# Gate projections of a hybrid layer: made among the attention heads and kept in DRAM, in place of all together behind them

## Chip, cores and metric

The program runs on one core of a Trainium2 chip (trn2). The metric is the device time of the whole program in microseconds: 1872.27 us in the kernel before, the median of three runs (1864.81 to 1877.15).

## What is computed

Two transformer blocks run one after the other on 512 tokens of width 1024, in float32. The change lies in the first half of the first block, which mixes tokens in two ways and weighs them with two gates:

```python
n = rmsnorm(h, g_mix)
z = n @ w_in                                     # 1024 -> 3*1536 + 512 + 2*1024
q, k, v, u = ...                                 # 12 heads of 128, and u of 512 channels
gate_attn = sigmoid(z[..., o2:o2 + 1024])
gate_ssm = sigmoid(z[..., o2 + 1024:o2 + 2048])
# 3 groups of 4 heads with dilations 1, 4 and 16; causal band in each; joined by their log-sums
attn_d = joined_heads @ w_attn_proj              # 512 -> 1024
y = gelu(s5_ssm(u, ...))                         # 32 groups of 16 channels, 64 complex states each
ssm_d = (y @ w_glu_a) * sigmoid(y @ w_glu_b)
h = h + (gate_attn * attn_d + gate_ssm * ssm_d) @ w_out
```

The feed-forward of block 1, the per-layer embedding and all of block 2 follow; the change does not touch them.

## The kernel before

Activations lie transposed, 128 channels by 512 tokens to a tile. Each float32 product is made of three matmuls on TensorE (PE): every operand is split into a high part, copied by ScalarE (ACT, L122), and a low part, the difference, made by VectorE (DVE, L123). `mm` (L159 to L161) issues high x high, high x low, low x high; where a row reads `mm<-y0h,wh`, the projection's input tile 0 meets the weight tile. One projection (`proj`) of 8 input tiles to 128 output channels is 24 matmuls of 512 columns. `weights` (L139 to L153) loads the 128 x 1024 weights of one projection into one of three buffers `wr` (L150) on the DMA queue of SyncE (SP), and splits them into one of two pairs `wh`/`wl`; the load and the split are given a priority 40 steps ahead of the place where they are called (`WLEAD`). A scheduler orders each engine's instructions by such priorities; each queue, SP's too, is served in order.

Block 1 first makes y (the input times the gain, split), u and the tables. Then four rounds `h` run `attention_1`, one head of each of the three groups in each: per group `qk_tile` for q and for k (projection, rotary embedding on DVE and GpSimd (POOL), split), a projection for v, its transposition (L703), scores (`sc`), masks and maxima, exponentials (L659 and L726 wait for such steps); at the end softmax weights, transposes of the probabilities (L736) and their products with v (`po`, L748; the copy into `attn` is L751). The last part of a head runs after the next head's first projection.

The state space (`ssm_work`, L502 to L606) is a generator of 4 groups `q` of four steps: load `u` (L517) and make phases; make 128-row blocks of weights and store `kd` (L548); 24 matmuls of 64 columns into a bank called `bu`, then a scan; load `kd` again in another order (L588), 48 matmuls of 64 columns into `bu`, gelu (L599), store `yd` (L601) and load it back as `ys` (L603). `SSM_RATE = (2, 2, 2)` takes two of the sixteen steps per group and head, so that heads 0 to 2 use them all up and head 3 runs without.

After the last head's products the loop at L835 makes the 16 gates: a projection each, a multiplication by the norm on DVE (L842) and a tanh on ACT (L843), each kept in a tile of its own. At L855 PSUM is divided anew (three banks `mm`, two `sc`), attention and state space outputs are split (`at`, `yss`), and eight merge steps `j` follow: three projections of half length on PE (`pp`, `pg`, `pg`, 36 matmuls), then on DVE, ACT and POOL the products with the gates (`ga`, `gs`) and a split (L872 to L877). Then come w_out and the norm; its residual tiles `res` are loaded from DRAM (L888).

Of the kernel before, what the change touches and what calls it, by code (L numbers as in the profile page):

```python
# [9 lines left out]
F32 = mybir.dt.float32  # L10
# [3 lines left out]
OP = mybir.AluOpType  # L14
# [23 lines left out]
SSM_RATE = (2, 2, 2)  # L38
# [46 lines left out]
class Program:  # L85
# [53 lines left out]
    def weights(self, ap, n, eng=None, pool=None, bufs=1, parts=1):  # L139

        r = self.t(self.wp, "wr", (128, 8, 128), F32, 3)
        if pool is None:
            h, l = self.pair(self.wp, "w", (128, 8, 128), 2)
        else:
            h, l = self.pair(pool, "ws", (128, n, 128), bufs)
        p0 = self.tc.cur_priority
        self.tc.cur_priority = max(0, p0 - WLEAD[self.phase])
        for i in range(0, n, n // parts):
            b = slice(i, i + n // parts)
            self.Q.dma_start(r[:, b], ap[:, b])  # L150
            self.last_split = self.split(h[:, b], l[:, b], r[:, b], eng)
        self.tc.cur_priority = p0
        return h, l  # L153
# [350 lines left out]
    def ssm_work(self, ap):  # L504
# [8 lines left out]
        for q in range(4):  # L513
            gr, cl = slice(8 * q, 8 * q + 8), slice(128 * q, 128 * q + 128)
            u = self.t(ap, "uy")
            for l in range(CH):
                Q.dma_start(n3(u[16 * l:16 * l + 16]),  # L517
                            self.ud[q].rearrange("(g c) (i n) -> i c g n", c=16, i=CH)[CH - 1 - l])
            uh, ul = self.split_new(ap, "us", u)
# [28 lines left out]
            Q.dma_start(self.kd[112:240, cl], dm.rearrange("p g c -> p (g c)"))  # L548
            wg = self.pair(ap, "wA", (128, 8, 128))
# [27 lines left out]
            hh, hl = self.split_new(ap, "hs", h)  # L577
            yield

            x, x2 = self.t(ap, "x", (128, 1024)), self.t(ap, "x2", (128, 1024))  # L580
# [5 lines left out]
            x = self.t(ap, "x", (128, 1024))  # L586
            for l in range(CH):
                Q.dma_start(x[16 * l:16 * l + 16].rearrange("p (j x) -> p j x", j=CH),  # L588
                            self.kd[16 * l:16 * l + 128, cl].rearrange("(j c) x -> c j x", c=16))
            wt = self.pair(ap, "wA", (128, 8, 128))  # L590
            self.split(*[w.rearrange("p g (j c) -> p g j c", c=16) for w in wt],
                       x.rearrange("p (j g c) -> p g j c", j=CH, c=16))
# [5 lines left out]
            y = self.t(ap, "uy")  # L598
            S.activation(y, p, AF.Gelu_apprx_tanh)  # L599
            yd = self.dp.tile([128, T], F32, name=f"yd{q}")  # L600
            Q.dma_start(yd, y)  # L601
            for g in range(8):
                Q.dma_start(self.ys[q][16 * g:16 * g + 16].rearrange("p (j n) -> p j n", j=CH),  # L603
                            yd.rearrange("(j c) (g n) -> g c j n", c=16, g=8)[g])
            yield

# [9 lines left out]
    def qk_tile(self, ap, n, tag, g):  # L616
        V = self.V
        p = self.ps("mm")
        self.proj(p, self.weights(self.d["w_in"][n], 8), 8, self.y)
        src = self.tokens(p[:], g)[1]  # L620
        cos, sin = (self.cosp, self.sinp) if g else (self.cosr, self.sinr)
        a = lambda x: x.rearrange("p (r i) -> p r i", r=DIL)
        t = self.t(ap, "tq", bufs=2)
        sh = self.t(ap, "tsh", (32, T))
        V.tensor_tensor(out=a(t[:]), in0=src, in1=a(cos[:]), op=OP.mult)
        V.stream_shuffle(a(sh[:]), src[0:32], list(range(16, 32)) + list(range(16)))  # L626
        (V if ROPE_DVE else self.G).tensor_tensor(out=sh, in0=sh, in1=sin, op=OP.mult)  # L627
        V.tensor_tensor(out=t[0:32], in0=t[0:32], in1=sh, op=OP.add)
        return self.split_new(ap, tag, t, bufs=2)
# [50 lines left out]

    def attention_1(self, ap, ap2, h):
# [8 lines left out]
        for g in range(3):  # L690
# [7 lines left out]
            vt = self.t(ap, "tq", bufs=2)  # L698
            a = lambda x: x.rearrange("p (r i) -> p r i", r=DIL)
            V.tensor_tensor(out=a(vt[:]), in0=self.tokens(p[:], g)[1], in1=a((self.rp if g else self.r1)[:]), op=OP.mult)  # L700
            p = self.ps("pt")
# [58 lines left out]
    def block_1(self):  # L760
# [61 lines left out]
        self.ssm = self.ssm_work(sp)  # L822
        rest = iter(())
        for h in range(4):
            head = self.attention_1(ap, ap2, h)
            next(head)
            next(rest, None)
            next(head)
            rest = head
            if h == 2:  # L830
                for _ in self.ssm:
                    pass
                ss_cm.__exit__(None, None, None)
                gg_cm, gg = self.open("gates", "right")
        next(rest)  # L835
        self.phase = 1
        gates = []
        for j in range(16):
            p = self.ps("mm")
            self.proj(p, self.weights(d["w_in"][40 + j // 2 + 8 * (j % 2)], 8), 8, self.y)  # L840
            a = self.t(gg, f"g{j}")
            V.tensor_tensor(out=a, in0=p, in1=self.r1, op=OP.mult)  # L842
            S.activation(a, a, AF.Tanh, scale=0.5)  # L843
            gates.append(a)
# [15 lines left out]
        for j in range(8):  # L860
            ga, gs = gates[2 * j:2 * j + 2]
# [17 lines left out]
        gg_cm.__exit__(None, None, None)  # L879
# [630 lines left out]
```

## Time and profile before

| | |
|---|---|
| median of three runs | 1872.27 us (1864.81 to 1877.15) |
| the execution that was profiled | 1869.56 us |
| its span, first to last instruction | 1867.8 us |
| mean clock granted to TensorE | 0.98 of full speed |
| PE busy | 96% of the span |
| attention heads, gates and merge of block 1 | 45 to 513 us |

Busy time is the time in which an engine worked on any instruction; the chain of work that ended last goes through PE for 69% of the span, through DVE for 12%. Times within the span start at its first instruction. A window's row gives busy microseconds of each engine with the number of instructions that began in it, and the clock granted to TensorE, 1.00 for 2.4 GHz and 0.50 for 1.2 GHz.

### The profile page before, as it was taken

How to read it: one execution, taken by the hardware profiler on the slowest of the kernel's cores; microseconds unless marked ns; L12 is line 12 of the kernel's file. 1: busy time of each engine (PE TensorE's matmuls, PEld its weight loads, DVE VectorE, ACT ScalarE, POOL GpSimd, SP SyncE). 2: the span in 40 equal slices, each digit the busy share in tenths (PEclk: the TensorE clock that was granted, in tenths of full speed). 3: DMA queues.
4: the chain of work that ended last, by engine and by line, in shares of the span. 5: the costliest groups of instructions: out<-in, count | busy, mean ns of one | idle time of the engine just before them, and what ended most of it. 6: DMA issues, size and time to landing. Idle time of an engine off the chain costs nothing.

```text
span 1867.8 us, 22362 instructions
## 1 busy us (share of the span) xinstructions
PE 1802.1 (96%) x8426; PEld 1488.1 (80%) x8426; DVE 1113.7 (60%) x1891; ACT 785.4 (42%) x1189; POOL 405.4 (22%) x277
## 2 busy tenths in 40 slices
PE   8989999999999999999999889999899999999998
PEld 6778888888888777888888767788688788888887
DVE  8866866544556777543355898667633576555323
ACT  4444544343333223322245677658323354444331
POOL 1654412100221111110033544021311211111000
PEclk9988999999999999999999999999999999999999
DMA  6222222242326887333353111132233423333332
GB/s 212 78 73 74 81 87 79 79 135 91 102 91 221 254 270 257 124 95 93 103 172 102 51 35 35 63 101 91 72 102 109 130 90 99 94 101 90 96 100 77
DMA packets 78908, 205.83 MB, mean 110 GB/s; under 512 B 18208, under 2 KB 25120, under 8 KB 78800
## 3 DMA queue, kind: packets, MB, share of 16 engines
q1 hardware_dynamic: 78800, 204.40, 34.7%
q8 instruction: 66, 1.08, 0.3%
q14 instruction: 42, 0.34, 0.1%
HBM read 197.06 MB, written 7.31 MB: 109 GB/s over the span
## 4 chain that ended last, share of the span: by engine, by line
PE 69%; DVE 12%; DMA 8%; issue 4%; ACT 3%; POOL 3%; SPq 1%; POOLq 0%; DVEq 0%; ACTq 0%
PE mm L161 12%; PE mm L159 12%; PE mm L160 12%; DMA wa<-in_w_ada 5%; PE sc L161 5%; PE sc L160 4%; PE sc L159 4%; PE po L161 2%; PE po L159 2%; PE po L160 2%; PE pt L161 2%; PE pt L160 2%; PE pt L159 2%; DVE wa L325 2%; DVE wl L123 2%
## 5 line engine op out<-in xcount | busy, mean ns | idle before, releaser
L122 ACT ACTIVATE wh<-wr 128x1024 fp32r<-128x1024 f32 (+3 forms) x295 | 300.1, 1017 | 579.3 <-PE mm L160 281.6
L123 DVE TENSOR_TENSOR wl<-wr,wh 128x1024 fp32r<-128x1024 f32 (+3 forms) x287 | 354.1, 1234 | 316.3 <-ACT wh L122 305.1
L918 POOL TENSOR_TENSOR fa<-fa,fb 128x512 f32<-128x512 f32 x22 | 40.0, 1818 | 214.2 <-DVE fb L917 187.6
L325 DVE CUSTOM_DVE_ANT_0 wa<-wa,ca 128x1024 f32<-128x1024 f32 x48 | 61.3, 1282 | 31.8 <-DMA wa<-in_w_ada 29.8
L1360 POOL TENSOR_TENSOR f<-f,f 128x512 f32<-128x512 f32 x22 | 29.3, 1334 | 205.6 <-DVE f L1357 168.8
L627 POOL TENSOR_TENSOR tsh<-tsh,sinp 32x512 f32<-32x512 f32 x16 | 41.3, 2584 | 91.0 <-DVE tsh L626 81.7
L202 POOL TENSOR_TENSOR acc<-acc,sq 128x512 f32<-128x512 f32 x28 | 42.3, 1523 | 80.8 <-ACT sq L201 80.8
L161 PE MATMUL mm<-y0h,wl 128*128 128x512 f32 x107 | 45.0, 421 | 7.8 <-DVE wl L123 7.2
L159 PE MATMUL mm<-y0h,wh 128*128 128x512 f32 x107 | 44.0, 411 | 8.2 <-ACT wh L122 6.1
L367 ACT ACTIVATE sm<-sm,st,cols 128x128 f32<-128x128 f32 (+1 forms) x64 | 41.5, 650 | 20.3 <-DVE st L366 16.5
L876 POOL TENSOR_TENSOR g<-g,g 128x512 f32<-128x512 f32 x8 | 17.3, 2166 | 148.8 <-DVE g L875 148.8
L159 PE MATMUL mm<-y1h,wh 128*128 128x512 f32 x107 | 43.5, 407 | 0.2 <-ACT y1h L789 0.2
L160 PE MATMUL mm<-y3l,wh 128*128 128x512 f32 x107 | 42.5, 397 | 1.0 <-DVE y3l L790 1.0
L160 PE MATMUL mm<-y1l,wh 128*128 128x512 f32 x107 | 43.2, 404 | 0.1
L160 PE MATMUL mm<-y4l,wh 128*128 128x512 f32 x107 | 42.6, 398 | 0.6 <-DVE y4l L790 0.6
L160 PE MATMUL mm<-y2l,wh 128*128 128x512 f32 x107 | 43.1, 403 | 0.0
L160 PE MATMUL mm<-y0l,wh 128*128 128x512 f32 x107 | 43.1, 403 | 0.0
L161 PE MATMUL mm<-y1h,wl 128*128 128x512 f32 x107 | 43.0, 402 | 0.0
L159 PE MATMUL mm<-y3h,wh 128*128 128x512 f32 x107 | 42.8, 400 | 0.0
L159 PE MATMUL mm<-y2h,wh 128*128 128x512 f32 x107 | 42.8, 400 | 0.0
L161 PE MATMUL mm<-y2h,wl 128*128 128x512 f32 x107 | 42.7, 399 | 0.0
L159 PE MATMUL mm<-y7h,wh 128*128 128x512 f32 x107 | 42.7, 399 | 0.0
(2180 smaller groups left out, 5599.1 us busy)
## 6 DMA issues: line engine op xcount, KB each, us to landing
wr<-in_w_in SPq DMA_DIRECT2D x86, 512.0 KB, 3.3
wa<-in_w_ada SPq DMA_DIRECT2D x48, 512.0 KB, 4.5
wr<-in_w_up SPq DMA_DIRECT2D x44, 512.0 KB, 3.5
wr<-in_w_fg SPq DMA_DIRECT2D x22, 512.0 KB, 4.4
wr<-in_w_fu SPq DMA_DIRECT2D x22, 512.0 KB, 4.0
wr<-in_w_out SPq DMA_DIRECT2D x16, 512.0 KB, 3.4
wr<-in_w_fd SPq DMA_DIRECT2D x16, 448.0 KB, 3.3
wr<-in_w_down SPq DMA_DIRECT2D x16, 448.0 KB, 3.3
```

The source lines that it names most:

```text
L122: i = self.S.activation(h, src, AF.Copy)
L123: (eng or self.V).tensor_tensor(out=l, in0=src, in1=h.bitcast(F32), op=OP.subtract)
L159: self.P.matmul(ps, lhsT=ah, rhs=bh, start=first and i == 0, stop=False)
L160: self.P.matmul(ps, lhsT=ah, rhs=bl, start=False, stop=False)
L161: self.last_mm = self.P.matmul(ps, lhsT=al, rhs=bh, start=False, stop=last and i == n - 1)
L202: self.G.tensor_tensor(out=acc, in0=acc, in1=q, op=OP.add)
L325: V.tensor_tensor_reduce(out=w, in0=w, in1=ca, op0=OP.mult, op1=OP.add, scale=1.0, scalar=0.0, accum_out=self.mod[:, n:n + 1])
L367: i = S.activation(sm[:, :w], sm[:, :w], AF.Exp, bias=st[:, 1:2], scale=scale, accum_out=st[:, 2:3])
L627: (V if ROPE_DVE else self.G).tensor_tensor(out=sh, in0=sh, in1=sin, op=OP.mult)
L876: G.tensor_tensor(out=ga, in0=ga, in1=gs, op=OP.add)
L918: G.tensor_tensor(out=a, in0=a, in1=b, op=OP.mult)
L1360: G.tensor_tensor(out=ab[0], in0=ab[0], in1=ab[1], op=OP.mult)
```

## The change

1. **Gates.** A new method `gate` makes one gate and hands its tile, now one of three `tq` buffers, to a list; `send_gates` stores the tiles of that list in DRAM (`gd`), each behind the last weight load issued by then (`issue_after`). `GATES` sets how many follow the v projection of each group and head: one in head 0, three in each of heads 1 to 3, ten in all. Three more come before the last head's softmax and products, three after. The merge loads a pair of gates in each of its eight steps, into two buffers each.
2. **State space.** `SSM_RATE` is (1, 2, 2): five steps a head, so the sixteen last into head 3. The load of `u` for the next group, the load of `kd` back and the load of `y` are issued a step earlier or in another place; `u`, `y` and the reloaded `kd` use other buffers, and the stores and loads of `y` stand behind a weight load.
3. The tag `tq` has three buffers in place of two.

No matmul is added or taken away, and the state space, the heads and the merge compute what they did.

```diff
@@ -35,7 +35,10 @@
 KLN = (2, 3)
 PIN = (13,)
 ROPE_DVE = 0
-SSM_RATE = (2, 2, 2)
+SSM_RATE = (1, 2, 2)
+
+GATES = ((0, 0, 1), (1, 1, 1), (1, 1, 1), (1, 1, 1))
+GATES_LAST = 3
 UPS = 3
 WLEAD = (40, 40, 40, 40, 40, 40, 40, 40, 0)
 LAT = (3, 4, 5, 0, 1, 2)
@@ -147,7 +150,7 @@
         self.tc.cur_priority = max(0, p0 - WLEAD[self.phase])
         for i in range(0, n, n // parts):
             b = slice(i, i + n // parts)
-            self.Q.dma_start(r[:, b], ap[:, b])
+            self.last_load = self.Q.dma_start(r[:, b], ap[:, b])
             self.last_split = self.split(h[:, b], l[:, b], r[:, b], eng)
         self.tc.cur_priority = p0
         return h, l
@@ -510,12 +513,25 @@
...
-        for q in range(4):
-            gr, cl = slice(8 * q, 8 * q + 8), slice(128 * q, 128 * q + 128)
-            u = self.t(ap, "uy")
+
+        def load_u(q):
+            u = self.t(ap, "u")
             for l in range(CH):
                 Q.dma_start(n3(u[16 * l:16 * l + 16]),
                             self.ud[q].rearrange("(g c) (i n) -> i c g n", c=16, i=CH)[CH - 1 - l])
+            return u
+
+        def load_y(q, yd):
+
+            with self.tc.issue_after(self.last_load.ins):
+                for g in range(8):
+                    Q.dma_start(self.ys[q][16 * g:16 * g + 16].rearrange("p (j n) -> p j n", j=CH),
+                                yd.rearrange("(j c) (g n) -> g c j n", c=16, g=8)[g])
+
+        u = load_u(0)
+        late = None
+        for q in range(4):
+            gr, cl = slice(8 * q, 8 * q + 8), slice(128 * q, 128 * q + 128)
...
@@ -546,6 +562,12 @@
...
             Q.dma_start(self.kd[112:240, cl], dm.rearrange("p g c -> p (g c)"))
+            xt = self.t(ap, "x2", (128, 1024))
+            for l in range(CH):
+                Q.dma_start(xt[16 * l:16 * l + 16].rearrange("p (j x) -> p j x", j=CH),
+                            self.kd[16 * l:16 * l + 128, cl].rearrange("(j c) x -> c j x", c=16))
+            if late:
+                load_y(*late)
             wg = self.pair(ap, "wA", (128, 8, 128))
...
@@ -575,34 +597,32 @@
...
+            if q < 3:
+                u = load_u(q + 1)
             yield
+            wt = self.pair(ap, "wA", (128, 8, 128))
+            self.split(*[w.rearrange("p g (j c) -> p g j c", c=16) for w in wt],
+                       xt.rearrange("p (j g c) -> p g j c", j=CH, c=16))
             x, x2 = self.t(ap, "x", (128, 1024)), self.t(ap, "x2", (128, 1024))
...
-            x = self.t(ap, "x", (128, 1024))
-            for l in range(CH):
-                Q.dma_start(x[16 * l:16 * l + 16].rearrange("p (j x) -> p j x", j=CH),
-                            self.kd[16 * l:16 * l + 128, cl].rearrange("(j c) x -> c j x", c=16))
-            wt = self.pair(ap, "wA", (128, 8, 128))
-            self.split(*[w.rearrange("p g (j c) -> p g j c", c=16) for w in wt],
-                       x.rearrange("p (j g c) -> p g j c", j=CH, c=16))
...
-            y = self.t(ap, "uy")
+            y = self.t(ap, "sa")
             S.activation(y, p, AF.Gelu_apprx_tanh)
             yd = self.dp.tile([128, T], F32, name=f"yd{q}")
-            Q.dma_start(yd, y)
-            for g in range(8):
-                Q.dma_start(self.ys[q][16 * g:16 * g + 16].rearrange("p (j n) -> p j n", j=CH),
-                            yd.rearrange("(j c) (g n) -> g c j n", c=16, g=8)[g])
+            late = q, yd
             yield
+            with self.tc.issue_after(self.last_load.ins):
+                Q.dma_start(yd, y)
+        load_y(*late)
...
@@ -620,7 +640,7 @@
...
-        t = self.t(ap, "tq", bufs=2)
+        t = self.t(ap, "tq", bufs=3)
...
@@ -678,6 +698,25 @@
...
+    def gate(self, ap, n):
+
+        self.send_gates()
+        for _ in range(n):
+            j = len(self.gd)
+            p = self.ps("mm")
+            self.proj(p, self.weights(self.d["w_in"][40 + j // 2 + 8 * (j % 2)], 8), 8, self.y)
+            a = self.t(ap, "tq", bufs=3)
+            self.V.tensor_tensor(out=a, in0=p, in1=self.r1, op=OP.mult)
+            self.S.activation(a, a, AF.Tanh, scale=0.5)
+            self.gd.append(self.dp.tile([128, T], F32, name=f"gd{j}"))
+            self.made.append((self.gd[j], a))
+
+    def send_gates(self):
+        for d, a in self.made:
+            with self.tc.issue_after(self.last_load.ins):
+                self.Q.dma_start(d, a)
+        self.made = []
+
...
@@ -695,9 +734,10 @@
             k = self.qk_tile(ap, 12 + 4 * g + h, "k", g)
             p = self.ps("mm")
             self.proj(p, self.weights(self.d["w_in"][24 + 4 * g + h], 8), 8, self.y)
-            vt = self.t(ap, "tq", bufs=2)
+            vt = self.t(ap, "tq", bufs=3)
             a = lambda x: x.rearrange("p (r i) -> p r i", r=DIL)
             V.tensor_tensor(out=a(vt[:]), in0=self.tokens(p[:], g)[1], in1=a((self.rp if g else self.r1)[:]), op=OP.mult)
+            self.gate(ap, GATES[h][g])
...
@@ -820,6 +860,7 @@
         a2_cm, ap2 = self.open("A2")
         ss_cm, sp = self.open("SS", "right")
         self.ssm = self.ssm_work(sp)
+        self.gd, self.made = [], []
         rest = iter(())
         for h in range(4):
             head = self.attention_1(ap, ap2, h)
@@ -827,21 +868,16 @@
             next(rest, None)
             next(head)
             rest = head
-            if h == 2:
-                for _ in self.ssm:
-                    pass
-                ss_cm.__exit__(None, None, None)
-                gg_cm, gg = self.open("gates", "right")
+        self.phase = 1
+        for _ in self.ssm:
+            pass
+        for _ in range(GATES_LAST):
+            self.gate(ap, 1)
         next(rest)
-        self.phase = 1
-        gates = []
-        for j in range(16):
-            p = self.ps("mm")
-            self.proj(p, self.weights(d["w_in"][40 + j // 2 + 8 * (j % 2)], 8), 8, self.y)
-            a = self.t(gg, f"g{j}")
-            V.tensor_tensor(out=a, in0=p, in1=self.r1, op=OP.mult)
-            S.activation(a, a, AF.Tanh, scale=0.5)
-            gates.append(a)
+        while len(self.gd) < 16:
+            self.gate(ap, 1)
+        self.send_gates()
+        ss_cm.__exit__(None, None, None)
...
@@ -858,7 +894,9 @@
             ys.append(self.pair(bp, f"yss{h}"))
             self.split(a(ys[h][0]), a(ys[h][1]), self.ys[h].rearrange("p (j n) -> p n j", j=CH))
         for j in range(8):
-            ga, gs = gates[2 * j:2 * j + 2]
+            ga, gs = self.t(bp, "ga", bufs=2), self.t(bp, "gs", bufs=2)
+            for x, n in ((ga, 2 * j), (gs, 2 * j + 1)):
+                Q.dma_start(x, self.gd[n])
...
```

In the order of TensorE's instructions, the second half of a state space group (48 `bu` matmuls) in head 0 stands in the kernel before behind the v projection, with only transposes and a score beside its first four; the next 44 follow one another:

```order
L161 MATMUL mm<-y7h,wl 128x512
L159 MATMUL bu<-hsh,wHh 128x64
L703 MATMUL pt<-ident,tq 128x128 x4
L159 MATMUL sc<-kh,qh 128x128
L545 MATMUL pt<-cc,x 128x16 x3
L160 MATMUL bu<-hsl,wHh 128x64
L161 MATMUL bu<-hsh,wHl 128x64
```

In the changed kernel a later group's `bu` matmuls, in head 1, alternate first with scores (`sc`) and then with the wide matmuls of a projection:

```order
L164 MATMUL sc<-kh,ql 128x128
L162 MATMUL bu<-ush,wAh 128x64
L163 MATMUL bu<-usl,wAh 128x64
L164 MATMUL bu<-ush,wAl 128x64
L162 MATMUL bu<-ush,wAh 128x64
L162 MATMUL mm<-y0h,wh 128x512
L163 MATMUL bu<-usl,wAh 128x64
L163 MATMUL mm<-y0l,wh 128x512
L164 MATMUL bu<-ush,wAl 128x64
L164 MATMUL mm<-y0h,wl 128x512
```

So most narrow matmuls moved in between wide ones; runs of 42 and of 44 `bu` matmuls in a row are left in the changed order.

On ScalarE, at the end of the heads, the kernel before has the splits of the outputs (`at0h` to `at3h`, `yss0h` to `yss3h`) behind the copy of the last head's output (L751), ahead of the tanh (L843) of most gates:

```order
L739 ACTIVATE pT<-pt 128x384
L122 ACTIVATE wh<-wr 128x1024
L751 ACTIVATE attn_88<-po 128x512
L122 ACTIVATE at0h<-attn_85 128x512
...
L122 ACTIVATE at3h<-attn_88 128x512
L843 ACTIVATE g_3639<-g_3639 128x512
L122 ACTIVATE wh<-wr 128x1024
```

In the changed kernel the same splits stand behind the tanh of the last gate (L710), and the merge's first sigmoid (L908) follows them:

```order
L125 ACTIVATE wh<-wr 128x1024
L710 ACTIVATE tq<-tq 128x512
L791 ACTIVATE attn_88<-po 128x512
L125 ACTIVATE at0h<-attn_85 128x512
...
L125 ACTIVATE yss3h<-ys_92 128x512
L908 ACT_TABLE_LOAD
L908 ACTIVATE gb<-sc 128x512
```

The copy of the last head's output has moved past the rest of the gates, to the merge's beginning.

On SP's queue the changed kernel begins the merge with the store of the last gate, the loads of the first two pairs of gates, and the `res` loads, which in the kernel before stood among the weight loads of the gates:

```order
L717 DMA gd_3974<-tq 128x512
L153 DMA wr<-in_w_glu 128x1024
L899 DMA ga<-gd_1149 128x512
L899 DMA gs<-gd_1500 128x512
L899 DMA ga<-gd_1734 128x512
L899 DMA gs<-gd_2028 128x512
L925 DMA res_4523<-in_xT 128x512
...
L153 DMA wr<-in_w_glu 128x1024
L899 DMA gs<-gd_2602 128x512
```

Before, no load but those of weights stood there:

```order
L150 DMA wr<-in_w_ap 128x1024
L150 DMA wr<-in_w_glu 128x1024 x2
L150 DMA wr<-in_w_ap 128x1024
```

The queue has gained a store or load of a gate between nearly every two weight loads of this stretch.

## Rows read from the trace of the kernel before

**Rows 1.** The page: busy time of each engine, and one of its costliest groups.
```profile
PE 1802.1 (96%) x8426; PEld 1488.1 (80%) x8426; DVE 1113.7 (60%) x1891; ACT 785.4 (42%) x1189; POOL 405.4 (22%) x277
...
L876 POOL TENSOR_TENSOR g<-g,g 128x512 f32<-128x512 f32 x8 | 17.3, 2166 | 148.8 <-DVE g L875 148.8
```

**Rows 2.** Windows: length, busy (count) of PE, PEld, DVE, ACT, POOL; clock; DMA share, GB/s.
```profile
45.00:116.00 71.00, 61.94 (x309) 49.39 (x307) 60.76 (x107) 32.83 (x50) 50.84 (x44) 1.00 0.23 72
116.00:133.00 17.00, 17.00 (x75) 16.52 (x76) 6.83 (x20) 6.35 (x13) 3.83 (x5) 0.50 0.30 94
133.00:167.20 34.20, 31.39 (x158) 25.54 (x157) 28.18 (x47) 14.65 (x19) 15.66 (x10) 1.00 0.24 72
167.20:177.40 10.20, 10.20 (x46) 9.64 (x45) 7.28 (x13) 3.43 (x6) 5.01 (x7) 0.50 0.32 103
177.40:228.60 51.20, 49.90 (x293) 43.37 (x291) 34.32 (x66) 28.38 (x48) 21.05 (x11) 1.00 0.24 69
228.60:238.90 10.30, 10.30 (x43) 9.69 (x43) 8.04 (x19) 3.93 (x6) 2.03 (x1) 0.50 0.22 76
238.90:296.90 58.00, 56.75 (x335) 49.59 (x334) 36.27 (x65) 24.56 (x39) 13.84 (x7) 1.00 0.27 84
296.90:300.30 3.40, 3.40 (x13) 3.01 (x13) 1.27 (x10) 0.18 (x1) 0.00 (x0) 0.50 0.28 95
300.30:398.60 98.30, 98.30 (x496) 83.26 (x495) 52.40 (x121) 37.46 (x67) 14.03 (x6) 1.00 0.25 83
398.60:447.90 49.30, 49.30 (x221) 40.83 (x220) 23.41 (x26) 20.07 (x27) 0.00 (x0) 1.00 0.43 139
447.90:513.20 65.30, 65.30 (x290) 54.08 (x289) 34.64 (x42) 23.82 (x30) 15.12 (x7) 1.00 0.29 97
```

**Rows 3.** Waits of PE from 58 to 118 us: sum, times, longest.
```profile
PE pt L703 <- DVE tq L700: 1.6, 2, 1.2
...
PE mm L161 <- DVE wl L123: 1.3, 2, 1.0
PE sc L159 <- DVE near L382: 1.0, 1, 1.0
```

**Rows 4.** The same, from 118 to 520 us.
```profile
PE pt L736 <- DVE sm L726: 2.5, 1, 2.5
PE pt L659 <- DVE ex L656: 1.3, 1, 1.3
```

**Rows 5.** Windows of tile bu alone: length, PE, PEld, DVE, ACT busy; clock; DMA.
```profile
116.00:125.40 9.40, 9.40 (x44) 9.40 (x44) 0.00 (x0) 0.00 (x0) 0.50 0.34 113
291.00:295.90 4.90, 4.90 (x44) 4.84 (x43) 0.00 (x0) 0.00 (x0) 1.00 0.30 110
```

**Rows 6.** Groups of ACT by line from 395 to 520 us.
```profile
L122 ACT ACTIVATE wh<-wr 128x1024 fp32r<-128x1024 f32 x22 | 23.3, 1061 | 50.4 <-issue 27.4 <-PE mm L160 12.5 <-PE sc L160 6.6
L843 ACT ACTIVATE g<-g 128x512 f32<-128x512 f32 x10 | 6.2, 618 | 1.0 <-DVE g L842 1.0
...
L870 ACT ACT_TABLE_LOAD x1 | 1.3, 1283 | 0.0
L122 ACT ACTIVATE yss0h<-ys 128x512 fp32r<-128x512 f32 x1 | 1.2, 1152 | 0.0
```

**Rows 7.** Tile at0h: duration in ns min/median/max, first and last start in us.
```profile
L122 ACT ACTIVATE at0h<-attn x1: 624/624/624, 399.4 to 399.4; 128x512 fp32r<-128x512 f32 x1
L123 DVE TENSOR_TENSOR at0l<-attn,at0h x1: 680/680/680, 400.9 to 400.9; 128x512 fp32r<-128x512 f32 x1
```

**Rows 8.** Timeline of PE at 337 us: start, length, instruction.
```profile
337.33 1.68 PE L748 MATMUL po<-pT,v 128*128 128x256 f32 x8
```

**Rows 9.** DMA issues: count, KB each, median us from issue to landing.
```profile
xd<-res SPq DMA_DIRECT2D x8, 256.0 KB, 2.2
...
res<-xd SPq DMA_DIRECT2D x8, 256.0 KB, 5.9
```

**Rows 10.** Waits of the DMA queue on SP from 45 to 330 us.
```profile
SPq L601 <- ACT uy L599: 28.9, 4, 10.0
```

More of the change, by code (lines that the diff above doesn't have):

```diff
@@ L878, in block_1 @@
         b_cm.__exit__(None, None, None)
-        gg_cm.__exit__(None, None, None)
         x1_cm.__exit__(None, None, None)
```

## Prediction

> **What bounds the kernel now.** I read the busy line first, then windows over the part that the change touches, then what PE waited for there. PE is busy 96% of the span, DVE 60%, and no other engine more [rows 1], so PE bounds. A change can win three things: time in which PE stands, time at the lower clock, or work taken off PE. This one takes no matmul away, which leaves two.
>
> The windows cut the stretch where the clock falls [rows 2]. From 45 to 447.9 us the attention heads run, then the gate projections; the merge follows until 513.2. PE stands 9.06 us before 116 (71.00 - 61.94), 2.81 up to 167.2, 1.30 up to 228.6, 1.25 up to 296.9, and never after that: 14.42 us in all. Four stretches, 17.0, 10.2, 10.3 and 3.4 us long, have a granted clock of 0.50, the lower level of 1.2 GHz: 40.9 us, in which PE does half of what it does at 2.4 GHz, so 20.45 us are lost. Standing and clock together cost 34.9 us, and that is all this change can reach.
>
> The cause is the mix. Until 116 us DVE is busy 60.76 of 71.00 us (86%) and POOL 50.84 (72%); from 300.3 to 398.6, where a head runs without the state space, DVE has 53%, and PE never stands [rows 2]. In the early part PE waits for DVE: for transposes of V, for split weights, for a free score bank [rows 3]; later for softmax results [rows 4]. The gate projections, 87 us of PE (16 x 24 matmuls at 0.227, the merge's 65.30 over its 288), leave DVE idle for more than half the time (23.41 of 49.30 us, other splits included) and stand at the end, where PE needs no filler [rows 2].
>
> **The clock.** The low stretch that begins at 116 us holds a run of 44 narrow matmuls (64 columns) of the state space, taking 9.40 us; a like run of 44 at 291 took 4.90 at full clock [rows 5], yet the clock fell right behind it, at 296.9, for 3.4 us [rows 2]. PE had not stood in those last 5 us. So runs of narrow matmuls without a projection between them bring the clock down, and standing adds to it. The skill has a rule on this. The Trainium skill (TensorE: Matmul & The Clock Gate, section HAM oscillation) ties the fall to idle gaps of PE. By that rule, runs of narrow matmuls alone would cost nothing; the run at 291 speaks against it, and what it would give is rival 1.
>
> **The change, part by part.** The sum is made against the profiled execution, 1869.56 us (span 1867.8); the median shown, 1872.27, lies 2.7 above, and the forecast is put on the median's scale.
>
> *Early standing.* PE's order is the same up to the third projection of the first head, so the first two waits stay: 0.4 of the 1.6 us for transposes and 1.0 of the 1.3 for split weights. I keep the third too, 1.0 for scores, whose matmul now stands twelve later [rows 3]: 2.4 us. Behind that the first head has a state space step fewer and a gate more, so DVE gets 5.4 us of PE time in which it needs less than half. I take 1.6 us as left of the other 6.7. Gain 5, with bounds of 2 (waits of other kinds come in their place) and 6.7.
>
> *Later standing.* 5.36 us, of which 3.8 are softmax waits [rows 4]. DVE's work from 45 to 447.9 sums to 259 us [rows 2] and is now spread: about 67% throughout, between the 53% at which PE never stood and the 73% (69.8 in 95.6 us) from 133 to 228.6 at which it stood 4.1. I take 2.4 left, gain 3; bounds -3 (as in that stretch, for twice as long) and 5.4.
>
> *Clock.* In the new order most narrow matmuls alternate with a projection's wide ones, and I count three runs that stay bare: 42 of them in head 1, 44 followed by 12 score matmuls and transposes, and some 29 mixed with softmax transposes. The two stretches of before whose runs had little or no standing in them were 10.3 and 3.4 us long [rows 2]; their mean, 6.85, three times, is 20.6 us, so 10.3 lost and 10.1 won. Bounds: 3 x 3.4 low, gain 15.3; 3 x 17.0 low, gain -5. I take the mean since nothing in the trace says on which side these three fall.
>
> *Start of the merge.* In before, the splits of the four attention tiles ran at 399 to 407 us, 48 us ahead of the merge [rows 7], under nine gates. Now head 3 ends beside the last gate, and ACT's order has the eight splits behind that gate's tanh. From the last gate's end PE has 1.68 us of `po` matmuls [rows 8]. Beside them ACT does a weight split (1.06) and a tanh (0.62) [rows 6]; then it copies attn3 (to 2.30) and splits at0 (0.62, to 2.92) [rows 7]: PE stands 1.25. The ys splits, 1.15 us each [rows 6], are then faster than the six matmuls that each feeds (1.36), but the first is some 0.65 late. If the gap brings the clock down for 3.4 us, 1.7 are lost; I take half of it: -1.25 - 0.65 - 0.85 = -2.75. Bounds: -1.25, and -5.3 (6.8 us low).
>
> *Gates by way of DRAM.* 16 stores and 16 loads of 256 KB. A like store took 2.2 us to land and a like load 5.9 [rows 9]; DMA is a quarter busy in the heads and 0.29 in the merge [rows 2]. A merge step takes 8.16 us (65.3 / 8). The buffer of step j is free 4.8 us after the step's end (two operations on DVE and one more behind ACT, 0.68 each, ACT's 0.62 [rows 7], POOL's 2.17 [rows 1]), the load lands at 10.7, and step j+2 first uses it at 8.16 + 2.7 = 10.9. If it is late, DVE waits, and PE only when the next score bank is due, 5.4 us on. Cost 0. The first pair is issued behind the last gate's store and lands some 8 us after that gate, when DVE has just done the splits. The eight `res` loads, 2 MB, that now stand between the first and later pairs can delay the third step's pair by a few us, within those 5.4.
>
> *ACT tables.* The tanh among exponentials makes 28 table loads from 24. At 1283 ns [rows 6] that is 5.1 us on an engine half idle: cost 0, bound -5.1. The Trainium skill (ScalarE: Activation LUTs, section What ACT_TABLE_LOAD costs) adds a drain, 2.66 us a switch. The trace agrees on the load and shows no drain apart; by the page the bound would be -10.6 and the sum the same.
>
> *State space loads.* `u` and `kd` come a step ahead and the store of `y` stands behind a weight load. SP's queue waited 28.9 us for that store, 10.0 at the longest [rows 10], and no wait of PE came from it: cost and gain 0.
>
> Sum: 5 + 3 + 10.1 - 2.75 = 15.35 us, 1854.2 beside the profiled run, 1856.9 on the median's scale: I forecast 1857. All best bounds (6.7 + 5.4 + 15.3 - 1.25 = 26.2) give 1846, all worst (2 - 3 - 5 - 5.3 - 5.1 = -16.4) 1889.
>
> **Rivals.** *1: the clock follows standing alone*, so filled runs keep it up: 20.45 in place of 10.1, gain 25.7, 1847. For it: standing comes before three of the four falls [rows 3, 4]. Against: the run at 291. The skill's rule named above would end here.
>
> *2: the loss moves.* DVE's total is unchanged; waits spread to heads 1 to 3, bare runs cost 10 us each, gain 0 to 7: 1865 to 1872, say 1868. For it: from 177.4 to 300.3 DVE was at 65% (79.9 in 122.9 us), no busier than it will be, and the clock fell twice [rows 2]. Against: PE never stood once DVE fell to 53%.
>
> *3: slower, through SP's queue.* SP is in order, and each gate's store waits for its tanh; the weight loads behind it wait too. It decides where a store holds the queue longer than the 10.0 us that were harmless [rows 10]. If half of the ten stores among the heads make PE stand 4 us and lower the clock for 3.4 (1.7 lost), that is 5 x 5.7 = 28.5 against 15.35 won: 1885. Against: a store stands behind the weight loads of the next group's three or four projections, some 16 us after its own.
>
> **How the numbers follow.** The forecast's case has 0.50, with its own range 1848 to 1865; rival 1 0.18, rival 2 0.23, rival 3 0.09. 8 in 10 need rivals 1 and 2 but not 3: 1842 to 1874. A measurement tells some 1% (18.7 us) from none. Faster by more: rival 1 and half of the forecast's case less a little, 0.42; slower by more: most of rival 3, 0.08; the rest, 0.50, within 1%.
>
> **What would show it.** Right: PE's standing from 45 us to the merge near 6 us, low clock near 20 us in two to four stretches, each at a bare `bu` run; a gap of 1 to 3 us on ACT's at0 split as the merge begins; no wait of PE behind `ga`. Wrong: low stretches gone (rival 1), as many as before (rival 2), or PE waiting on ACT's wh split behind a late weight load (rival 3); or a merge step longer than 8.2 us, which would put a price on the loads.

## The result, and the profile after

The changed kernel takes 1857.8 us (14 runs, 1855.21 to 1861.12), the kernel before 1867.36 over 14 runs (1861.79 to 1877.15). The ratio is 0.9946 (0.9933 to 0.9959): 10.1 us less (7.7 to 12.5). The profiled executions differ by 9.2 us, 1869.56 and 1860.36. The page of the changed kernel begins:

```profile
PE 1792.3 (96%) x8426; PEld 1477.7 (80%) x8426; DVE 1114.9 (60%) x1891; ACT 789.4 (42%) x1193; POOL 398.1 (21%) x277
```

PE has as many instructions as in [rows 1] and is busy 9.8 us less. The work is the same, so most of that is clock: half of the low time that is gone in the part that the change touches makes some 5 us of it, and some 3 us lie outside that part, where the span changes by 0.5 us. The windows of the changed kernel, with the columns of [rows 2]:

```profile
45.00:62.10 17.10, 16.61 (x76) 13.34 (x74) 14.57 (x36) 8.36 (x11) 10.55 (x15) 1.00 0.21 76
62.10:123.60 61.50, 59.14 (x323) 49.28 (x321) 51.15 (x90) 32.68 (x52) 35.53 (x32) 1.00 0.33 96
123.60:130.50 6.90, 6.90 (x22) 5.78 (x22) 3.32 (x13) 5.46 (x7) 0.64 (x1) 0.51 0.27 93
130.50:195.30 64.80, 62.35 (x334) 53.24 (x332) 41.41 (x74) 24.76 (x41) 21.57 (x12) 1.00 0.29 89
195.30:205.60 10.30, 7.84 (x18) 5.70 (x19) 9.93 (x12) 3.35 (x5) 6.47 (x6) 0.50 0.16 51
205.60:212.40 6.80, 6.80 (x55) 6.46 (x54) 1.92 (x2) 3.28 (x4) 0.89 (x2) 1.00 0.39 130
212.40:226.10 13.70, 13.70 (x49) 12.16 (x49) 2.44 (x13) 6.05 (x13) 0.40 (x1) 0.50 0.35 103
226.10:300.00 73.90, 72.05 (x390) 61.44 (x390) 53.20 (x94) 33.08 (x50) 23.50 (x12) 1.00 0.25 81
300.00:437.60 137.60, 136.21 (x716) 115.96 (x714) 75.96 (x157) 54.30 (x89) 20.22 (x11) 1.00 0.32 104
```

Length less PE's busy time is standing: 0.5 + 2.4 up to 123.6, then 8.15 up to 437.6 (2.45 + 2.46 + 1.85 + 1.39). Three stretches are at 0.50, 30.9 us together, where before there were four with 40.9. What PE waited for, from 119 to 440 us, which answers to [rows 4] (sum, times, longest):

```profile
PE mm L162 <- ACT wh L125: 3.0, 1, 3.0
PE sc L162 <- DVE near L385: 1.8, 2, 1.2
PE bu L162 <- ACT hsh L125: 1.8, 1, 1.8
PE mm L162 <- DVE sv L597: 1.2, 1, 1.2
PE sc L162 <- ACT at0h L125: 1.2, 1, 1.2
PE sc L163 <- DVE at0l L126: 0.2, 1, 0.2
```

Neither wait of [rows 4] is left; others stand in their place. In windows of the tile `bu` alone (columns of [rows 5]), the two bare runs that were still at full clock when the fall came:

```profile
119.40:123.50 4.10, 4.10 (x38) 4.10 (x38) 0.00 (x0) 0.00 (x0) 1.00 0.18 53
207.40:212.20 4.80, 4.80 (x44) 4.80 (x43) 0.00 (x0) 0.00 (x0) 1.00 0.21 65
```

The clock falls at 123.6 and 212.4, right behind. The third fall, at 195.3, has no such run ahead of it but the standing for `wh`.

### The profile page after: what moved, and what is told of

It reads as the page before. It is cut to its first block, busy times and chain, and to the rows that moved or that the text cites. A ratio compares the mean times of both kernels' runs of the same rounds, so it can differ in the third digit from the quotient of the medians.

```text
span 1858.6 us, 22464 instructions
## 1 busy us (share of the span) xinstructions
PE 1792.3 (96%) x8426; PEld 1477.7 (80%) x8426; DVE 1114.9 (60%) x1891; ACT 789.4 (42%) x1193; POOL 398.1 (21%) x277
## 4 chain that ended last, share of the span: by engine, by line
PE 70%; DVE 12%; DMA 7%; issue 5%; POOL 3%; ACT 2%; SPq 0%; POOLq 0%; DVEq 0%; ACTq 0%
PE mm L164 13%; PE mm L162 13%; PE mm L163 13%; DMA wa<-in_w_ada 5%; PE sc L164 5%; PE sc L162 5%; PE sc L163 5%; PE po L164 2%; PE po L162 2%; PE po L163 2%; PE pt L164 2%; PE pt L163 2%; PE pt L162 2%; DVE wl L126 2%; DVE wa L328 2%
## 5 line engine op out<-in xcount | busy, mean ns | idle before, releaser
L126 DVE TENSOR_TENSOR wl<-wr,wh 128x1024 fp32r<-128x1024 f32 (+3 forms) x287 | 358.7, 1250 | 313.1 <-ACT wh L125 309.5
L328 DVE CUSTOM_DVE_ANT_0 wa<-wa,ca 128x1024 f32<-128x1024 f32 x48 | 61.1, 1273 | 32.8 <-DMA wa<-in_w_ada 30.9
L647 POOL TENSOR_TENSOR tsh<-tsh,sinp 32x512 f32<-32x512 f32 x16 | 37.2, 2327 | 101.2 <-DVE tsh L646 101.2
L164 PE MATMUL mm<-y0h,wl 128*128 128x512 f32 x107 | 45.9, 429 | 10.3 <-DVE wl L126 10.1
L162 PE MATMUL mm<-y0h,wh 128*128 128x512 f32 x107 | 44.4, 415 | 10.3 <-ACT wh L125 9.1
L164 PE MATMUL mm<-y3h,wl 128*128 128x512 f32 x107 | 42.8, 400 | 0.0
L162 PE MATMUL mm<-y4h,wh 128*128 128x512 f32 x107 | 42.8, 400 | 0.0
```

The costliest lines, as they stand in the source:

```text
L126: (eng or self.V).tensor_tensor(out=l, in0=src, in1=h.bitcast(F32), op=OP.subtract)
L162: self.P.matmul(ps, lhsT=ah, rhs=bh, start=first and i == 0, stop=False)
L164: self.last_mm = self.P.matmul(ps, lhsT=al, rhs=bh, start=False, stop=last and i == n - 1)
L328: V.tensor_tensor_reduce(out=w, in0=w, in1=ca, op0=OP.mult, op1=OP.add, scale=1.0, scalar=0.0, accum_out=self.mod[:, n:n + 1])
```

## The experiments

For all kernels the same stretch was taken from the traces, from the fourth projection of the first round of heads (at some 55 us) to the first matmul of w_out: its length, the standing in heads and at the merge's start (gaps between PE's instructions), and the time at low clock. The ratio is to the kernel before on the same chip, with its interval, over all executions; the other columns are us in the one execution that was profiled. That one can lie off the median, from 3.7 us under it (splits_early) to 6.5 over it (rate_112).

| kernel | ratio | stretch | standing heads | merge | low |
|---|---|---|---|---|---|
| before | 1 | 458.3 | 14.4 | 0 | 41.0 |
| changed | 0.9946 (0.9933 to 0.9959) | 449.6 | 11.0 | 1.4 | 30.7 |
| gates_end | 1.0006 (0.9986 to 1.0025) | 458.0 | 14.9 | 2.3 | 37.5 |
| rate_222 | 1.0000 (0.9983 to 1.0016) | 457.1 | 17.5 | 1.4 | 37.5 |
| dram_only | 0.9990 (0.9973 to 1.0007) | 458.3 | 13.0 | 0 | 44.4 |
| old_loads | 0.9922 (0.9897 to 0.9946) | 449.0 | 7.7 | 1.4 | 37.5 |
| narrow_spread | 0.9952 (0.9936 to 0.9968) | 448.2 | 13.8 | 1.4 | 20.5 |
| narrow_added | 1.0092 (1.0075 to 1.0109) | 475.0 | 11.4 | 1.4 | 51.2 |
| splits_covered | 0.9971 (0.9957 to 0.9985) | 452.6 | 13.1 | 3.5 | 23.9 |
| splits_early | 0.9923 (0.9902 to 0.9944) | 448.7 | 11.9 | 0 | 30.7 |
| phase_after_hs | 0.9964 (0.9949 to 0.9979) | 452.8 | 14.9 | 1.4 | 30.7 |
| rope_on_dve | 0.9899 (0.9881 to 0.9916) | 439.9 | 4.1 | 1.4 | 27.3 |
| combined | 0.9906 (0.9888 to 0.9924) | 438.9 | 10.8 | 0 | 10.2 |
| rate_112 | 0.9953 (0.9936 to 0.9969) | 453.3 | 14.8 | 4.7 | 27.3 |

The stretch less all standing less half the low time is 419 to 424 us in every row but narrow_added (436.5, with 14.7 us of added work). So these two losses account for the differences of the stretch to some 2 us either way. The low time of a single execution is a small sample, but the mean granted clock of all executions goes the same way: 0.979 before, 0.984 changed, 0.986 in narrow_spread, 0.988 in combined, 0.976 in narrow_added. In splits_covered it is 0.982, so the 23.9 us of its row flatter it.

**Which part brings the gain.**

```diff
-GATES = ((0, 0, 1), (1, 1, 1), (1, 1, 1), (1, 1, 1))
-GATES_LAST = 3
+GATES = ((0, 0, 0), (0, 0, 0), (0, 0, 0), (0, 0, 0))
+GATES_LAST = 0
```

> The changed kernel with GATES all zero and GATES_LAST = 0: the sixteen gates stand behind the last head again, still kept in DRAM; the state space stays spread and its loads ahead. Theory (the gates' wide matmuls among the heads are what fills PE and separates the narrow runs): the standing of PE from 62 us to the end of the heads goes back from 11 us to about 14, the low clock from 31 us to about 40, time 1863 to 1868 us against 1857.8 of the changed kernel. Rival (the spread of the state space and its earlier loads bring the gain, wherever the gates stand): standing 9 to 11 us, low clock about 31 us, 1856 to 1860 us.

```diff
-SSM_RATE = (1, 2, 2)
+SSM_RATE = (2, 2, 2)
```

> The changed kernel with SSM_RATE = (2, 2, 2) as before: gates among the heads, state space not spread into head 3. Theory (gates carry the gain): 1857 to 1862 us, standing within 2 us of the changed kernel's 11. Rival (the spread carries it): 1863 us or more, standing 13 us or more and low clock 40 us as in the kernel before.

Measured: 1866.76 and 1867.16 us beside 1866.4 of the kernel before. Either part without the other brings nothing that shows. The first theory held for gates_end and fell for rate_222: gates among the heads don't carry the gain alone. In rate_222 the longest wait is 4.98 us; the timeline around it (start, length, engine, instruction):

```profile
100.53 2.10 POOL L647 TENSOR_TENSOR tsh<-tsh,sinp 32x512 f32<-32x512 f32 x1 [2.55 <-DVE tsh L646]
...
101.41 5.27 DVE L126 TENSOR_TENSOR wl<-wr,wh 128x1024 fp32r<-128x1024 f32 x1
...
102.59 1.25 POOL L511 TENSOR_TENSOR sa<-sv,tc 128x512 f32<-128x512 f32 x1
103.79 0.59 POOL L547 COPY rt<-rho 128x504 f32<-128x504 f32 x1
...
104.35 1.25 POOL L511 TENSOR_TENSOR sb<-sb,ts 128x512 f32<-128x512 f32 x1
...
106.74 0.80 PE L164 MATMUL mm<-y0h,wl 128*128 128x512 f32 x1 [4.98 <-DVE wl L126]
```

A weight split that takes 1.2 us took 5.27 while POOL ran four instructions end to end, and PE waited for it. That led to rope_on_dve, below.

**The way through DRAM.** The kernel before with

```diff
-            a = self.t(gg, f"g{j}")
+            a = self.t(gg, "g", bufs=3)
...
-            gates.append(a)
+            gates.append(self.dp.tile([128, T], F32, name=f"gd{j}"))
+            Q.dma_start(gates[-1], a)
...
-            ga, gs = gates[2 * j:2 * j + 2]
+            ga, gs = self.t(bp, "ga", bufs=2), self.t(bp, "gs", bufs=2)
+            for x, n in ((ga, 2 * j), (gs, 2 * j + 1)):
+                Q.dma_start(x, gates[n])
```

> The kernel before with one edit: the sixteen gates, made where they were, are stored in DRAM and loaded back in the merge, two buffers each as in the changed kernel. Theory (the way through DRAM costs nothing): 1864 to 1869 us beside 1866.4 of the kernel before, 8.16 us for a merge step, no wait of PE that the kernel before doesn't have. Rival (the loads are late for the products of a step, or the stores hold the weight loads behind them): a merge step of 8.5 us or more, 1870 us or more.

Measured 1866.4 us, beside 1868.65 of the kernel before on the same chip. Its merge, as a window to lay beside the last line of [rows 2]:

```profile
446.30:511.60 65.30, 65.30 (x290) 54.11 (x289) 34.65 (x42) 23.79 (x30) 15.00 (x7) 1.00 0.45 150
```

The same 65.30 us without a gap, DMA at 0.45 in place of 0.29: the way through DRAM costs the merge nothing that shows.

**The loads of the state space.** `ssm_work` of the changed kernel replaced by that of the kernel before.

> The changed kernel with the state space's generator of the kernel before: loads of u and kd and the store and loads of y where they stood. Gates among the heads and SSM_RATE = (1, 2, 2) stay. Theory (the earlier loads cost and bring nothing): 1855 to 1861 us. Rival (they are what makes the spread pay, since a load that is late holds a step and the work queued behind it): 1863 us or more, with waits of PE for tiles of the state space (us, wA, bu) that the changed kernel doesn't have.

Measured 1854.7 us. The early loads bring nothing; whether they cost a few us stays open, since the intervals of this ratio and of the changed kernel's touch and the stretches are 449.0 and 449.6.

**The clock.** First the narrow runs taken apart:

```diff
+                p0 = self.tc.cur_priority
+                self.tc.cur_priority = p0 + 40 + 30 * g
                 self.mm(p[:, n], [((wt[0][:, g], wt[1][:, g]), (uh[:, n], ul[:, n])),
                                   ((wh[0][:, g], wh[1][:, g]), (hh[:, n], hl[:, n]))])
+                self.tc.cur_priority = p0
```

> The changed kernel with one edit: the 48 narrow matmuls of a group's second half get later and later priorities (40 + 30 per sixth), so that at most 23 of them stand in a row in PE's order in place of 44. Theory (a bare run of some 44 narrow matmuls brings the clock down, without any standing): the low stretches at 124 and 212 us go (6.8 and 13.7 us long, half of it lost), the one behind the standing at 193 us may stay: low clock about 10 us in the heads in place of 31, time about 1848 us (1846 to 1852). Rival (standing alone brings it down): low clock 25 to 35 us, time 1856 to 1860 us.

Measured 1855.6 us. Neither expectation held. Its windows at low clock:

```profile
122.10:125.50 3.40, 3.40 (x10) 2.90 (x11) 1.63 (x4) 0.63 (x1) 1.01 (x1) 0.50 0.40 142
...
197.20:204.00 6.80, 5.81 (x14) 4.53 (x15) 6.80 (x10) 2.21 (x3) 3.45 (x3) 0.50 0.24 77
...
258.70:265.50 6.80, 5.82 (x17) 4.38 (x17) 6.80 (x11) 2.80 (x5) 2.88 (x2) 0.50 0.00 0
...
306.40:309.80 3.40, 3.40 (x10) 2.71 (x10) 1.47 (x11) 1.73 (x7) 0.00 (x0) 0.51 0.42 155
```

No stretch of 13.7 us is left. The first three begin behind standing of 1.8, 2.4 and 3.4 us (`ex`, `wh`, `sm` in its waits). The last begins behind neither standing nor a bare `bu` run, but behind 4 us of scores and transposes (16 to 128 columns) with single `bu` matmuls between them. So falls follow standing too, as at 195.3 in the changed kernel, where wide matmuls stood ahead of it; no run adds standing alone. New waits took back what the spreading won: the ratio is no other than the changed kernel's. Then the converse, narrow runs added where PE hardly stands:

```diff
+            if h == 3 and g > 0:
+                p = self.ps("bu")
+                for i in range(44 if g == 1 else 88):
+                    self.P.matmul(p[:, 64 * (i % 8):64 * (i % 8) + 64], lhsT=q[0][:, :128], rhs=k[0][:, :64], start=True, stop=True)
```

> The changed kernel with narrow matmuls added where PE hardly stands: 44 and then 88 matmuls of 64 columns, one run each, behind the gates of the second and third group of head 3 (about 360 to 430 us); their result is not used. At full clock they take 132 x 0.111 = 14.7 us. Theory (a bare run of narrow matmuls brings the clock down without standing): a low stretch in or right behind at least one of the two, where the changed kernel has none between 340 and 440 us; time 1876 to 1886 us. Rival (standing alone does): no low stretch there, 1872 to 1873 us.

Measured 1883.5 us. The windows of that part:

```profile
340.00:377.40 37.40, 37.40 (x238) 33.53 (x237) 17.64 (x36) 15.39 (x26) 4.21 (x2) 1.00 0.34 111
377.40:384.20 6.80, 6.80 (x24) 5.83 (x24) 0.93 (x8) 0.60 (x1) 0.00 (x0) 0.50 0.02 5
384.20:408.10 23.90, 23.90 (x128) 20.51 (x126) 11.19 (x16) 6.03 (x7) 4.22 (x2) 1.00 0.26 86
408.10:425.20 17.10, 17.10 (x75) 16.34 (x75) 1.26 (x10) 2.50 (x9) 0.00 (x0) 0.50 0.05 19
```

And the tile `bu` alone, up to the two falls:

```profile
372.00:377.40 5.40, 5.00 (x44) 4.88 (x43) 0.00 (x0) 0.00 (x0) 1.00 0.72 239
403.70:408.10 4.40, 4.40 (x41) 4.40 (x40) 0.00 (x0) 0.00 (x0) 1.00 0.37 107
```

PE stands nowhere here, and yet the clock falls at each run: for 6.8 us behind the 44 matmuls, and for 17.1 us within the 88, behind the first 41. The stretch is 25.4 us longer than the changed kernel's: 14.7 of added work and half of 20.5 more at low clock. The trace of before could only suggest this.

**The merge's start.** First the last six gates called behind the last head's products, in tiles of their own:

```diff
-GATES_LAST = 3
+GATES_LAST = 0
...
+        ss_cm.__exit__(None, None, None)
+        gg_cm, gg = self.open("gates", "right")
         while len(self.gd) < 16:
-            self.gate(ap, 1)
+            self.gate(gg, 1)
...
-        ss_cm.__exit__(None, None, None)
...
```

> The changed kernel with GATES_LAST = 0 and the last six gates in tiles of a pool of their own: the last gate's matmuls then stand behind the last head's products, and the splits of at and yss ahead of its tanh on ScalarE. Theory (PE stands at the merge's start because these splits come last): no wait of PE for at0 (1.2 and 0.2 us in the changed kernel), merge begins some 1.9 us sooner, 1856 us. Rival (the first merge step is held by something else, a late load of a gate or of weights): the wait moves to another tile and the time stays at 1858 us.

Measured 1861.57 us: the wait moved, from at0 to 2.1 us for the split of at3, which now stood behind those of yss on ScalarE. In TensorE's order only five matmuls of the last gate came to stand behind the products, too few to cover the splits. So the splits were put apart:

```diff
+        ss_cm.__exit__(None, None, None)
+        gg_cm, gg = self.open("gates", "right")
+        at = [self.split_new(gg, f"at{h}", self.attn[h]) for h in range(3)]
...
+            ys.append(self.pair(gg, f"yss{h}"))
...
         next(rest)
+        at.append(self.split_new(gg, "at3", self.attn[3]))
```

> The changed kernel with the splits of at0 to at2 and of yss ahead of the last head's products, in a pool of their own that is free by then; at3 alone is split behind the copy of the last head's output. Theory (PE stands at the merge's start for those splits alone): no wait of PE for at0 (1.2 + 0.2 us in the changed kernel), the ys splits hold nothing either, the merge begins 1.9 us sooner: 1856 us (1854 to 1858). Rival (splits put earlier take ScalarE and VectorE time that the last gates or the softmax need): new waits of 1 us or more between 400 and 437 us and no gain, 1858 us or more.

Measured 1854.78 us; no wait of PE is left from 400 to 500 us, as expected. How much time that brings isn't clear: the interval of its ratio overlaps the changed kernel's, and the stretch is 0.9 us shorter.

**The waits at 193 to 199 us.**

```diff
+            with self.tc.issue_after(last_hs.ins) if q else ExitStack():
                 S.activation(co, ph, AF.Abs, scale=TURN)
...
```

> The changed kernel with one edit in the state space: the three activations that make the next group's cosine and sine (tc, ts) are queued on ScalarE behind the split hs of the group before. In the changed kernel PE stands 3.0 and 1.8 us at 193 to 199 us for a weight split (wh) and for hs that are queued on ScalarE behind the activation into tc, which waited for GpSimd's last use of the old tc; a low stretch of 10.2 us begins there. Theory (that queue order is the cause, and standing of some us brings the clock down too): both waits and that low stretch go, 4.8 + 5.1 = 9.9 us, time 1848 us (1846 to 1853). Rival (the weight split is late by itself, its load or its buffer): the wait stays near 3 us and the time at 1856 to 1860 us.

Measured 1861.44 us, no faster than the changed kernel (the intervals overlap), so the expectation failed. The wait for `wh` fell to 1.5 us, and one of 4.9 for DVE's half of the split came behind it:

```profile
PE mm L164 <- DVE wl L126: 5.0, 2, 4.9
```

VectorE, busy without a break from 189 to 201 us, was late, not the queue of ScalarE alone. From its timeline there:

```profile
189.11 2.32 DVE L650 TENSOR_TENSOR tq<-tq,tsh 32x512 f32<-32x512 f32 x1 [1.16 <-POOL tsh L649]
...
193.75 2.40 DVE L126 TENSOR_TENSOR ql<-tq,qh 128x512 fp32r<-128x512 f32 x1
196.08 2.28 DVE L511 TENSOR_TENSOR x<-ar,bb 128x1024 f32<-128x1024 f32 x1
198.28 1.21 DVE L126 TENSOR_TENSOR wl<-wr,wh 128x1024 fp32r<-128x1024 f32 x1
```

VectorE first waits for GpSimd's rotary product, and then three of its instructions take some 2.3 us where 0.7, 0.7 and 1.2 are usual. That product was then moved to VectorE:

```diff
-ROPE_DVE = 0
+ROPE_DVE = 1
```

> The changed kernel with the rotary product of 32 rows on VectorE in place of GpSimd (ROPE_DVE = 1). At 185 to 200 us operations of the two engines stretch each other (GpSimd's product took 4.36 us where 1.7 was its shortest; VectorE's additions 2.3 to 2.4 where 0.7 is usual). Theory (that stretching makes VectorE late there): the standing of 3.0 + 1.8 us at 193 to 199 and the low stretch behind it go, up to 9.9 us, 1848 to 1854 us. Rival (24 products more on VectorE cost more than the stretching): new standing in the first heads, 1860 us or more.

Measured 1847.66 us, 19 us less than the kernel before (15.7 to 22.2): 24 instructions that changed their engine add some 9 us to what the change brought. All that PE waited for from 58 to 440 us:

```profile
PE bu L162 <- ACT hsh L125: 1.6, 1, 1.6
PE mm L162 <- ACT wh L125: 1.3, 1, 1.3
PE sc L162 <- ACT at0h L125: 1.2, 1, 1.2
PE mm L164 <- DVE wl L126: 0.8, 1, 0.8
PE sc L162 <- DVE near L385: 0.3, 1, 0.3
PE sc L163 <- DVE at0l L126: 0.2, 1, 0.2
```

Standing in the heads falls from 11.0 to 4.1 us, though VectorE has more to do. The two waits for `wh` and `hs`, 3.0 and 1.8 us in the changed kernel, are 1.3 and 1.6, not gone, and the clock still falls there; the rest came from waits elsewhere.

The edit does two things at once, and which of them pays isn't shown. It takes work off GpSimd, which stretches VectorE's instructions and is stretched by them, and it spares VectorE the wait for the product. In the changed kernel from 55 to 440 us that wait was

```profile
DVE tq L648 <- POOL tsh L647: 18.2, 15, 2.5
```

and the product on VectorE takes a third of its median time on GpSimd (2111 ns, last section):

```profile
L647 DVE TENSOR_TENSOR tsh<-tsh,sinp x16: 669/673/2421, 63.5 to 378.1; 32x512 f32<-32x512 f32 x16
```

Stretched instructions of VectorE are not fewer: of the forms that occur three times or more, those over a quarter longer than the shortest of their form are 16 in the changed kernel and 19 here, and what the instructions beside a working GpSimd took beyond their shortest fell from 21.3 to 19.5 us only. At the place of the longest waits (185 to 198 us in the changed kernel) it fell by half, from 4.5 to 2.2 us. So less stretching is not shown to be what pays; the sparing of the wait is a rival, and a run that removes the one without the other is missing.

**Together.** The edits of old_loads, splits_early and narrow_spread in one kernel, and the same with `SSM_RATE = (1, 1, 2)`:

> The changed kernel with three edits at once: the generator of the kernel before (old places of the loads), the splits of at0 to at2 and yss ahead of the last head's products, and the second half's narrow matmuls at later priorities (at most 24 in a row). Theory (the losses are apart and add): merge's start 1.9 us, clock 2 to 10 us, loads 0 to 3 us: 1845 to 1853 us where the changed kernel has 1857.8. Rival (each edit only moves the losses): 1854 us or more, with standing and low clock together no less than the changed kernel's.

> The combined kernel with SSM_RATE = (1, 1, 2): four steps a head, so that the state space runs evenly through all four heads. Theory (PE stands where a head's share of state space steps fills VectorE): standing before the merge under 7 us, low clock under 20 us, 1843 to 1850 us. Rival (one group's steps are a burst however they are spread): standing 9 us or more, 1853 us or more.

Measured 1848.74 and 1858.36 us. Combined, inside the range of its first theory, the low time falls to 10.2 us and the merge starts without a gap. The even spread fell short: three waits of 3.1 to 3.5 us, one a head, and 4.7 at the merge, where the last y comes back from DRAM late and a gate's product stands behind its split on VectorE. A group's steps are a burst, however the steps are counted per head.

## Why the prediction was right, and where it was not

The time, the range and the side came out; the gain was 10.1 us and not 15.35. That 1857 lies so near 1857.8 is luck: three runs gave 1872.27 for the kernel before, fourteen 1867.36, and this error of the base cancels that of the gain. Two of the signs that the prediction named did not come: standing near 6 us (it was 11.0) and low clock near 20 us, each at a bare run (30.9, one of them behind standing).

- *What bounds:* held. Standing and clock account for the stretch of all kernels above, to some 2 us.
- *Early standing:* gain 5 forecast; 9.06 us became 2.85, gain 6.2.
- *Later standing:* gain 3 forecast; 5.36 us became 8.15, a loss of 2.8, at the bound of -3. The step that failed is "DVE's work is now spread: about 67% throughout". The mean was near (253.9 of 392.6 us, 65%), the spreading was not: in slices of 25 us from 50 us on VectorE's busy share runs from 38% to 94%, and every wait of PE above 0.9 us among the heads lies in a slice of 80% or more. Nor did the forecast see what fills them further: VectorE's own instructions are longer when GpSimd is at work, and it waits for GpSimd's products.
- *Clock:* gain 10.1 forecast from three bare runs of 6.85 us; 30.9 us were low, gain 5.0. The mis-sized term is the 6.85 us a run: at two of the named runs the clock fell, for 6.9 and 13.7 us, at the third, of 29, it did not, and a stretch of 10.3 us came from standing instead.
- *Merge start:* -2.75 forecast, -1.9 measured: 1.2 of waiting for at0 and a merge of 66.0 us in place of 65.3. The clock did not fall, and the first ys split was not late. splits_early shows the cause.
- *DRAM:* 0 forecast, and shown for the merge by dram_only. *State space loads:* 0 to a small loss. *ACT tables:* not tried alone.

The emptiest and the fullest of those slices, with the columns of [rows 2]:

```profile
200.00:225.00 25.00, 25.00 (x113) 22.12 (x112) 9.59 (x23) 9.96 (x17) 5.99 (x7) 0.64 0.35 109
250.00:275.00 25.00, 23.15 (x123) 19.34 (x122) 23.62 (x27) 12.94 (x21) 14.56 (x8) 1.00 0.18 61
```

The terms that the rows show, 6.2 - 2.8 + 5.0 - 1.9, make 6.5 of the 8.7 us by which the stretch is shorter. The rest is not in gaps: by clock and merge PE's busy time in the stretch would fall by 4.6 us, it fell by 6.7, and why isn't shown.

Rival 1 (standing alone moves the clock) fell with narrow_added; with it the Trainium skill's account (TensorE: Matmul & The Clock Gate, section HAM oscillation), which names idle gaps only, is incomplete for this kernel. Rival 2 (the waits move) was true of the later heads, not of the first. Rival 3 did not come: SP's queue waited 15 times for a gate's tanh, at most 6.9 us, and no wait of PE came from it.

## What to carry to other kernels

Filler work helps where the engine that PE waits for is full, so read busy shares in slices of a burst's length, not of a head's. A run of dozens of narrow matmuls is dear beyond its columns: put wide ones between them, and look which waits come of it (narrow_spread alone won nothing). Before moving work among engines, look whether the late engine's own instructions are longer than the shortest of their form, which engine works beside them, and for whom the late engine waits itself.

## What the hardware showed

VectorE and GpSimd stretch each other. In the changed kernel, durations of one form (tiles `tq` and `tsh`, 55 to 440 us; min/median/max in ns):

```profile
L648 DVE TENSOR_TENSOR tq<-tq,tsh x23: 671/678/2308, 59.0 to 390.6; 32x512 f32<-32x512 f32 x23
L645 DVE TENSOR_TENSOR tq<-mm,cosp x16: 667/686/693, 65.2 to 387.0; 128x512 f32<-128x512 f32 x16
...
L647 POOL TENSOR_TENSOR tsh<-tsh,sinp x16: 1283/2111/4360, 68.6 to 388.4; 32x512 f32<-32x512 f32 x16
```

The operation with two inputs in SBUF reaches 3.4 times its shortest, the one that reads PSUM never changes, and GpSimd's product reaches 4.36 us for 1.28 (not 1.7, as an expectation above has it). Of VectorE's forms that occur three times or more, 16 instructions took over a quarter longer than their shortest, all beside a working GpSimd; of 180 without it, none did. By the Trainium skill (SBUF — State Buffer, section Who interferes with whom), a VectorE instruction with two SBUF inputs contends with a GpSimd instruction that reads SBUF. The trace agrees, and rate_222 puts a price on it: 5.27 us for 1.2, when four GpSimd instructions come end to end.
